# Turning 32x32 blocks on VectorE and the rest by transfers, in place of TensorE transposes, in a FoX and RWKV-7 hybrid layer

## The chip, the core and the metric

The kernel runs on one core of a Trainium2 chip. The core's engines are named as in the profile: PE (TensorE; PEld is its weight load), DVE (VectorE), ACT (ScalarE), POOL (GpSimd) and SP (SyncE, which here only issues DMA transfers). 16 DMA engines move data between DRAM and the core's SBUF. The metric is the device time of one execution in microseconds (us), as a median of several; lower is better.

## The reference

One layer for 256 tokens of width 4096, in float32. One projection feeds two groups of heads and a gate, and their gated outputs go through a second projection into a LayerNorm residual:

```python
proj = jnp.einsum('bsd,dc->bsc', x, w_in)            # 4096 -> 16,592 columns
# 16 FoX heads of 128: causal softmax attention with a forget gate
logits = jnp.einsum('bhqd,bhkd->bhqk', qb, kf) + cb[..., :, None] - c[..., None, :]
out = jnp.einsum('bhqk,bhkd->bhqd', softmax(where(causal, logits, -inf)), vf)
# 32 RWKV-7 heads of 64: r, k, v are shifted by a token (a lerp with the token before), then per frame
sa = jnp.einsum('bhvk,bhk->bhv', state, a_t)
state = state * w_t[:, :, None, :] + sa[..., None] * b_t[:, :, None, :] + v_t[..., None] * k_t[:, :, None, :]
y_t = jnp.einsum('bhvk,bhk->bhv', state, r_t)
# GroupNorm of y per head, plus the bonus sum(r*k*r_k) * v
h = jnp.concatenate([fox_out, rwkv_out], -1) * silu(z)
x = layernorm(ALPHA * x + h @ w_out)
```

## The kernel before

**The projections.** The tokens are the matmul's stationary operand, in two halves of 128 (x, split into a high and a low part in fp32r), and the weights stream through. A weight tile w_q is 128x1024 float32, 512 KB: two steps of the contraction for 512 columns. SP fetches it (`fetch`, L215; 4 buffers), ACT rounds it to its high part (L138; 4 buffers), DVE subtracts to get the low part (L139; 3 buffers), and PE runs 12 matmuls on it (L144 to L146: high times high, low of x times high, high of x times low). Sixteen such tiles make a block of 512 columns for all 256 tokens, accumulated in two PSUM banks `acc`. The 16 groups of heads are taken as 8 pairs n, each with four blocks b: block 0 holds r and k of both groups of the pair, block 1 v of RWKV and v of FoX, blocks 2 and 3 q, k and the two gates of the even and of the odd group. The output projection (L784 to L786) is built alike from 128 tiles `wo`.

**The side work.** Everything else is written as generators that are resumed in slots: `slot()` is called every six matmuls, twice in a weight tile, and lets each of them go on to its next `yield`. `wait(n)` lets n slots pass, so the table `W` fixes how far apart in PE's stream the steps of a chain stand. The framework then orders each engine's instructions by when its own cost model has them ready, with program order as priority; `keep_in_program_order` pins one. Each engine and SP's DMA queue works its list strictly in order, so an instruction that waits holds those behind it.

**Where tiles are turned.** A block comes out of PE with tokens on the partitions; the recurrence and attention want channels there. `unload` (L721) turns the copy `bk` by TensorE transposes against the identity into PSUM tiles `tr` (L735), four per group, and ACT and DVE read those: `shifted` (L270) makes r, k and v with the token shift, L746 and L749 take q and k of a FoX head, `silu2` (L347) the gates. v is made a second time with tokens on the partitions (`vs`, L829 to L831 and L493 to L495) by a copy through DRAM one row apart and three POOL operations.

**The recurrence** (`rwkv`, L476) of a pair: Gram products `gp` (L488); their masked parts go through DRAM (nd, L509, eight transfers, and Nb, L510, two of 512 KB) into the layout of a triangular solve on DVE of 31 rows, each one product and one reduction (L536, L539); BK, the update's factors, is turned by eight transposes `tp` (L525) and copied by ACT (L526); the inverse goes back through DRAM (td, T; L545, L547), and a chunked sweep of PE steps follows. `bon`, the bonus, is multiplied by v (L517) ahead of the solve.

**Attention** (`fox`, L663): scores (L672, L673), softmax on DVE and ACT in `lg` (L678 to L682), three transposes `fpt` of the probabilities (L686), a copy to `pT` (L688), the product with v (L692).

Of the kernel before, what the change touches and what calls it, by code (L numbers as in the profile page):

```python
# [22 lines left out]
C = 64  # L23
NCH = S // C
# [15 lines left out]
BACK = 10  # L40
ROWS = 1
LAG = 2
BLOCKS = [[(0, 0), (1, 0), (0, 1), (1, 1)], [(2, 0), (2, 1)], [(3, 0), (4, 0), (5, 0), (6, 0)], [(3, 1), (4, 1), (5, 1), (6, 1)]]
W = {"fo": 3, "vs": 2, "np": 6, "gp": 5, "tp": 4, "d1": 8, "d2": 12, "xp": 3, "fs": 4, "fp": 5}
NB = D // OB

# [2 lines left out]
B = 32  # L49
# [33 lines left out]
def layer(ctx: ExitStack, tc: tile.TileContext, xt, xtok, w_lora, w_main, muv, w_o, up, par, mulora, fbias, lng, lnb, cst, out):  # L83
    nc = tc.nc
# [8 lines left out]
    def pst(name):  # L93
        return ps.tile([P, 512], F32, tag="ps", name=name)
# [37 lines left out]
    def column(name, i):  # L132
        return prm[:, PAR.index(name), i : i + 1]
# [124 lines left out]
    def t256(tag, name, bufs=1):  # L258
        return rp.tile([P, S], F32, tag=tag, name=name, bufs=bufs)
# [7 lines left out]

    vv = {}

    def shifted(p, n, i):  # L270
        name = f"s{n}_{i}"
        if n == 2:
            if i % 2 == 0:
                vv[i // 2] = rp.tile([P, 2, S], F32, tag="s2", name=name)
            r = vv[i // 2][:, i % 2, :]
        else:
            r = t256(f"s{n}", name, 2)
        lerp(p, prm[:, 7 + n, i : i + 1], omm[:, n, i : i + 1], r)
        return r

# [66 lines left out]
    def silu2(z, key):  # L347
        th = t256("zt", key + "t")
        nc.scalar.activation(th, z, AF.Tanh, scale=0.5)
        sz = t256("sz" + key[0], key + "s", 2 if key[0] == "r" else 1)  # L350
        nc.vector.scalar_tensor_tensor(sz, th, 1.0, z, ALU.add, ALU.mult)
        szs[key] = sz

    def gate(y, key, k):
        far = k < FAR
# [17 lines left out]
    def flat(t):  # L373
        return t.rearrange("p a b -> p (a b)")
# [3 lines left out]
    bks = {}  # L378
    muvs = {}
    turned = set()  # L380
    pairs = {}
    done = set()
    prepared = set()
# [91 lines left out]

    def rwkv(n):  # L476
        i0 = 2 * n
        while i0 + 1 not in prepared or n not in vv:
            yield
        q = pairs[n]  # L480
        lc, BK, lt, bon = q["lc"], q["BK"], q["lt"], q["bon"]
# [7 lines left out]
        v = vv[n]  # L489
# [27 lines left out]
        nc.vector.tensor_tensor(flat(bon), flat(bon), flat(v), ALU.mult)  # L517
        for u in range(2):
            nc.scalar.activation(bon[:, u], bon[:, u], AF.Identity, bias=column("gn_bias", i0 + u))
        yield from wait(W["tp"])  # L520
        BKt = rp.tile([P, 2, NCH, P], F32, tag="shl", name=f"BKt{n}")
        for u in range(2):
            tp = pst(f"tp{n}_{u}")
            for c in range(NCH):
                nc.tensor.transpose(tp[:, c * P : (c + 1) * P], BK[:, u, c, :], ident)  # L525
# [8 lines left out]
        for t, s in enumerate(range(B - 2, -1, -1)):  # L534
            w = B - 1 - s
            first = nc.vector.tensor_tensor(prod[:, :, :, s + 1 :], nb[:, :, s : s + 1, s + 1 :].to_broadcast([P, 2, NJ, w]), xc[:, :, :, s + 1 :], ALU.mult)  # L536
            if not t:
                tc.keep_in_program_order(first)
            nc.vector.tensor_reduce(xc[:, :, :, s : s + 1], prod[:, :, :, s:], AX.X, ALU.add)  # L539
            if t % ROWS == ROWS - 1:  # L540
                yield
        td = dram.tile([2, 4, NCH, B, B], F32, tag="td", name=f"td{n}", bufs=2)
# [120 lines left out]
    def fox(i, q, k, vt):  # L663
# [13 lines left out]
        for m, blk in enumerate((slice(0, 1), slice(1, 3))):  # L677
            nc.vector.scalar_tensor_tensor(lg[:, blk, :], spv[:, blk, :], ct[:, m * NF + i : m * NF + i + 1], nb[:, blk, :], ALU.add, ALU.add)  # L678
            nc.vector.tensor_reduce(st[:, m : m + 1], lg[:, blk, :], AX.XY, ALU.max, negate=True)
            nc.scalar.activation(lg[:, blk, :], lg[:, blk, :], AF.Exp, bias=st[:, m : m + 1], accum_out=st[:, 2 + m : 3 + m])  # L680
            nc.vector.reciprocal(st[:, 4 + m : 5 + m], st[:, 2 + m : 3 + m])
            nc.vector.tensor_scalar(lg[:, blk, :], lg[:, blk, :], st[:, 4 + m : 5 + m], None, ALU.mult)  # L682
        yield from wait(W["fp"])
        pt = pst(f"fpt{i}")
        for m in range(3):
            nc.tensor.transpose(pt[:, m * P : (m + 1) * P], lg[:, m, :], ident)  # L686
        pT = rp.tile([P, 3 * P], F32, tag="nb", name=f"pT{i}")
        nc.scalar.copy(pT, pt[:, : 3 * P])  # L688
        yield from wait(W["fo"])
        op = pst(f"fop{i}")  # L690
        f = slice(i % 2 * P, i % 2 * P + P)
# [22 lines left out]

    zero = rp.tile([1, 2 * P], F32, tag="prod", name="zero")
    nc.gpsimd.memset(zero, 0.0)
    vds = [dram.tile([S + 1, 2 * P], F32, name=f"vd{j}") for j in range(2)]
    for vd in vds:
        nc.sync.dma_start(out=vd[0:1], in_=zero)

    def unload(n, b, bk, vt):  # L721
        yield from wait(LAG)
        if b == 0:
            while n and 2 * n - 1 not in prepared:
                yield
        elif b == 2:
            while n and n - 1 not in done:
                yield
        fq = fk = None
        cols = BLOCKS[b]  # L730
        for h in range(len(cols) // 2):
            tr = pst(f"tr{n}_{b}_{h}")
            for t in range(2):
                for m in range(2):
                    nc.tensor.transpose(tr[:, t * S + m * P : t * S + (m + 1) * P], bk[:, m, (2 * h + t) * P : (2 * h + t + 1) * P], ident)  # L735
            for t in range(2):
                p = tr[:, t * S : (t + 1) * S]
                j, u = cols[2 * h + t]
                i = 2 * n + u
                if j < 3:  # L740
                    rk[i, j] = shifted(p, j, i)
                elif j == 3:
                    while i and i - 1 not in foxed:
                        yield
                    fq = t256("fq", f"fq{i}")
                    nc.scalar.mul(fq, p, FOX_SCALE)  # L746
                elif j == 4:
                    fk = t256("fk", f"fk{i}")
                    nc.scalar.copy(fk, p)  # L749
                    side(fox(i, fq, fk, vt))  # L750
                else:
                    silu2(p, f"fr"[j - 5] + str(i))
            yield
        unloading.clear()

    def get_h(k):
        assert k in kept_h
# [54 lines left out]
    for n in range(G // 2):  # L812
        for b in range(4):
# [12 lines left out]
            if b == 1:  # L826
# [10 lines left out]
            unloading.append(n)  # L837
            side(unload(n, b, bk, vt))

    closed.append(1)  # L840
    oacc = {}
# [174 lines left out]
```

## Time and profile before

| | |
|---|---|
| median of 3 runs | 1968.98 us (1968.77 to 1969.45) |
| the profiled execution's own time | 1967.9 us |
| its span, first to last instruction | 1966.1 us |
| mean granted TensorE clock | 0.999 |
| PE busy | 1955.8 us, 99% |
| DVE busy | 1351.5 us, 69% |
| ACT busy | 999.5 us, 51% |
| POOL busy | 81.0 us, 4% |
| DMA: bytes, packets | 392.86 MB, 146,383 |

How to read the rows that follow. A row of groups has line, engine, operation, output<-inputs and shapes, count, then busy time and mean ns of one, then idle time before it with what ended it. A row of a tile's view has count, then shortest, median and longest ns. A row of waits has who waited for whom, us in total, times, the longest. A time line has start and duration in us, and in brackets the idle time before it. A row of stretches has each engine's busy time and count, the granted clock, the mean busy share of the 16 DMA engines, and GB/s. The ends of matmuls are modelled; starts are recorded.

### The profile page before, as it was taken

What the parts mean: (1) busy time and instruction counts of PE and PEld (TensorE: products, weight loads), DVE (VectorE), ACT (ScalarE), POOL (GpSimd) and SP (SyncE); (2) the same over time, 40 slices, a digit from 0 to 9 for tenths busy, and PEclk for the clock granted to TensorE, in tenths of its full rate; (3) what the DMA queues carried; (4) which work ended last, traced back from release to release, by engine and by line L of the source; (5) the groups of instructions that cost most, each with busy time, mean ns of one, the idle gap of its engine ahead of it and who ended that gap; (6) DMA issues with size and microseconds to landing.
All of it is one profiled execution on the core that took longest, in us unless ns stands there. A gap on an engine that the chain in (4) does not pass through costs nothing.

```text
span 1966.1 us, 28320 instructions
## 1 busy us (share of the span) xinstructions
PE 1955.8 (99%) x10377; PEld 1608.1 (82%) x10377; DVE 1351.5 (69%) x2168; ACT 999.5 (51%) x1509; POOL 81.0 (4%) x111
## 2 busy tenths in 40 slices
PE   9999999999999999999999999999999999999998
PEld 8888788878887888788878887888788878888886
DVE  6688576857685768576857685778576856755555
ACT  6544564456445644564456445644564454444332
POOL 0110001000100010001000100010001000000000
PEclk9999999999999999999999999999999999999999
DMA  9566567656665666566656665676566787866664
GB/s 337 153 204 192 174 192 201 198 172 192 194 198 178 192 201 201 168 191 196 200 176 193 198 195 177 192 209 187 174 190 198 242 281 240 250 200 200 193 199 165
DMA packets 146383, 392.86 MB, mean 200 GB/s; under 512 B 32642, under 2 KB 48020, under 8 KB 146244
## 3 DMA queue, kind: packets, MB, share of 16 engines
q1 hardware_dynamic: 145812, 390.63, 65.4%
q8 instruction: 81, 1.33, 0.3%
q14 instruction: 58, 0.48, 0.1%
q10 hardware_dynamic: 432, 0.43, 0.1%
HBM read 374.98 MB, written 16.01 MB: 199 GB/s over the span
## 4 chain that ended last, share of the span: by engine, by line
PE 98%; DVE 1%; ACT 0%; issue 0%; ACTq 0%; DVEq 0%
PE acc L144 24%; PE acc L146 24%; PE acc L145 24%; PE oacc L784 6%; PE oacc L786 6%; PE oacc L785 6%; PE tr L735 1%; PE yp L634 1%; PE gp L488 1%; PE up L609 1%; PE rh L582 1%; PE sp L618 0%; PE accl L146 0%; PE accl L144 0%; PE accl L145 0%; PE tp L525 0%
## 5 line engine op out<-in xcount | busy, mean ns | idle before, releaser
L539 DVE TENSOR_REDUCE xc<-prod 128x8 f32<-128x16 f32 (+30 forms) x248 | 73.1, 295 | 6.0
L536 DVE TENSOR_TENSOR prod<-Nb,xc 128x8 f32<-128x8 f32 (+30 forms) x248 | 72.3, 292 | 7.1
L139 DVE TENSOR_TENSOR w_11l<-w,w_11h 128x1024 fp32r<-128x1024 f32 x31 | 37.9, 1223 | 39.0 <-ACT w_11h L138 20.4
L139 DVE TENSOR_TENSOR w_6l<-w,w_6h 128x1024 fp32r<-128x1024 f32 x31 | 38.0, 1226 | 37.0 <-ACT w_6h L138 17.5
L139 DVE TENSOR_TENSOR w_1l<-w,w_1h 128x1024 fp32r<-128x1024 f32 x31 | 37.9, 1223 | 35.9 <-PE acc L146 35.7
L139 DVE TENSOR_TENSOR w_0l<-w,w_0h 128x1024 fp32r<-128x1024 f32 x31 | 37.9, 1223 | 33.8 <-PE acc L146 22.3
L138 ACT CAST w_1h<-w 128x1024 fp32r<-128x1024 f32 x31 | 32.7, 1055 | 55.4 <-PE acc L145 37.6
L139 DVE TENSOR_TENSOR w_3l<-w,w_3h 128x1024 fp32r<-128x1024 f32 x31 | 37.8, 1221 | 31.8 <-PE acc L146 31.8
L138 ACT CAST w_2h<-w 128x1024 fp32r<-128x1024 f32 x31 | 32.7, 1056 | 48.8 <-PE acc L145 42.1
L138 ACT CAST w_11h<-w 128x1024 fp32r<-128x1024 f32 x31 | 32.5, 1050 | 46.5 <-DMA w<-in_w_main_dram 29.2
L138 ACT CAST w_0h<-w 128x1024 fp32r<-128x1024 f32 x31 | 32.7, 1055 | 43.5 <-PE acc L145 34.9
L139 DVE TENSOR_TENSOR w_2l<-w,w_2h 128x1024 fp32r<-128x1024 f32 x31 | 37.9, 1222 | 22.6 <-PE acc L146 22.4
L144 PE MATMUL acc<-w_4h,x 128*128 128x512 f32 x124 | 53.0, 427 | 0.0
L139 DVE TENSOR_TENSOR w_15l<-w,w_15h 128x1024 fp32r<-128x1024 f32 x31 | 37.9, 1221 | 21.6 <-PE acc L146 20.2
L139 DVE TENSOR_TENSOR w_9l<-w,w_9h 128x1024 fp32r<-128x1024 f32 x31 | 38.0, 1226 | 21.1 <-ACT pT L688 15.3
L138 ACT CAST w_13h<-w 128x1024 fp32r<-128x1024 f32 x31 | 32.7, 1054 | 37.5 <-DMA w<-in_w_main_dram 21.6
L139 DVE TENSOR_TENSOR w_14l<-w,w_14h 128x1024 fp32r<-128x1024 f32 x31 | 38.0, 1225 | 19.7 <-PE acc L146 9.0
L138 ACT CAST w_4h<-w 128x1024 fp32r<-128x1024 f32 x31 | 32.7, 1055 | 36.7 <-PE acc L145 36.7
L144 PE MATMUL acc<-w_1h,x 128*128 128x512 f32 x124 | 51.2, 413 | 0.0
L144 PE MATMUL acc<-w_6h,x 128*128 128x512 f32 x124 | 51.2, 413 | 0.0
L144 PE MATMUL acc<-w_2h,x 128*128 128x512 f32 x124 | 51.1, 412 | 0.0
L139 DVE TENSOR_TENSOR w_5l<-w,w_5h 128x1024 fp32r<-128x1024 f32 x31 | 43.5, 1403 | 10.9 <-PE acc L146 10.9
(836 smaller groups left out, 6592.9 us busy)
## 6 DMA issues: line engine op xcount, KB each, us to landing
w<-in_w_main_dram SPq DMA_DIRECT2D x496, 512.0 KB, 3.7
wo<-in_w_o_dram SPq DMA_DIRECT2D x128, 512.0 KB, 3.6
Nb<-nd SPq DMA_DIRECT2D x16, 512.0 KB, 5.8
wr<-in_w_main_dram SPq DMA_DIRECT2D x15, 512.0 KB, 6.4
hd<-hl SPq DMA_DIRECT2D x29, 256.0 KB, 4.4
h<-hd SPq DMA_DIRECT2D x29, 256.0 KB, 6.5
res<-in_xtok_dram SPq DMA_DIRECT2D x16, 256.0 KB, 4.7
xr<-in_xt_dram SPq DMA_DIRECT2D x15, 256.0 KB, 6.4
```

What stands on the lines that cost most here:

```text
L138: nc.scalar.copy(hi[:, :n], src[:, :n])
L139: nc.vector.tensor_tensor(lo[:, :n], src[:, :n], hi[:, :n].bitcast(F32), ALU.subtract)
L144: nc.tensor.matmul(acc[:, :n], xs[k][:, 0, tt], hi[:, o : o + n], start=(k == 0), stop=False)
L145: nc.tensor.matmul(acc[:, :n], xs[k][:, 1, tt], hi[:, o : o + n], start=False, stop=False)
L146: nc.tensor.matmul(acc[:, :n], xs[k][:, 0, tt], lo[:, o : o + n], start=False, stop=(k == KT - 1))
L488: nc.tensor.matmul(gp[u][j][:, c * P : (c + 1) * P], BK[h, u, c, :], lt[j][h, u, c, :], start=True, stop=True)
L536: first = nc.vector.tensor_tensor(prod[:, :, :, s + 1 :], nb[:, :, s : s + 1, s + 1 :].to_broadcast([P, 2, NJ, w]), xc[:, :, :, s + 1 :], ...
L539: nc.vector.tensor_reduce(xc[:, :, :, s : s + 1], prod[:, :, :, s:], AX.X, ALU.add)
L582: nc.tensor.matmul(rh[HALF[j], u * C : (u + 1) * C], lt[j][:, u, c, 0:C], SV[j][:, u, c, :], start=True, stop=True)
L784: nc.tensor.matmul(acc, ht[k][:, 0, tt], hi, start=(k == 0), stop=False)
L785: nc.tensor.matmul(acc, ht[k][:, 1, tt], hi, start=False, stop=False)
L786: nc.tensor.matmul(acc, ht[k][:, 0, tt], lo, start=False, stop=(k == KT - 1))
```

## The change

A 128-wide transpose is taken apart: DVE turns each 32x32 block within its own 32 partitions, and a transfer through DRAM moves the blocks to their places. The new helper `turn` writes a DVE-turned tile to DRAM with four transfers, one for each group of 32 partitions, in runs of 32 floats; reading the DRAM tile with partition = (block, row) gives the turned tile, in rows of 1 KB and more.

```diff
+    def turn(src, name):
+        _, m, cols = src.shape
+        d = dram.tile([cols // B, B, m, 4, B], F32, tag=f"dt{m}_{cols}", name=name, bufs=2)
+        s = src.rearrange("p m (q t) -> p m q t", t=B)
+        for a in range(4):
+            nc.sync.dma_start(out=d[:, :, :, a, :].rearrange("q i m t -> i m q t"), in_=s[B * a : B * (a + 1)])
+        return d
...
+    def turned_back(d):
+        return d.rearrange("(u b) i m a t -> u (b i) (m a t)", b=4).rearrange("u p s -> p u s")
```

**Projected blocks** 0, 2 and 3 go this way, except blocks 2 and 3 of the last pair, which keep the PE transposes. Block 3 starts 13 slots later (`BEHIND`). After the read-back, three slots (`LAND`) pass before r and k are shifted, two before attention starts; each group's r and k are read back together.

```diff
+        last = n == G // 2 - 1 and b > 1
+        if b == 3 and not last:
+            yield from wait(BEHIND)
+        if not last:
+            for m in range(2):
+                nc.vector.transpose(bk[:, m, :], bk[:, m, :])
+            yield
+            d = turn(bk, f"bt{n}_{b}")
+            unloading.clear()
+            yield
+        if b == 0:
+            for u in range(2):
                 i = 2 * n + u
+                while n and n - 1 not in bonned:
+                    yield
+                raw = rp.tile([P, 2, S], F32, tag="s2", name=f"raw{i}")
+                nc.sync.dma_start(out=raw, in_=turned_back(d[8 * u : 8 * u + 8]))
+                yield from wait(LAND)
+                for j in range(2):
+                    rk[i, j] = shifted(raw[:, j, :], j, i)
+            return
...
+            for j, t in enumerate((fq, fk, zf, zr)):
+                nc.sync.dma_start(out=t, in_=d[4 * j : 4 * j + 4].rearrange("b i m a t -> (b i) (m a t)"))
+                if j % 2:
+                    yield
+            yield from wait(LAND - 1)
+        nc.scalar.mul(fq, fq, FOX_SCALE)
+        side(fox(i, fq, fk, vt))
+        yield
+        silu2(zf, f"f{i}")
+        silu2(zr, f"r{i}")
```

**v** is no longer shifted a second time: block 1 has no `unload` any more, and the token-major `vs` is turned during the solve (rows 6, 8 and 10: `V_AT`), with UV as scratch. The bonus product and its two ACT operations move from ahead of the solve to its row 14.

```diff
+            if t == V_AT:
+                vst = UV[0].rearrange("p u c v -> p (u c v)").rearrange("p (m q) -> p m q", m=2)
+                for a in range(2):
+                    tc.keep_in_program_order(nc.vector.transpose(vst[:, a, :], vs_[n][:, a, :]))
+            if t == V_AT + 2:
+                vdr = turn(vst, f"vt{n}")
+            if t == V_AT + 4:
+                vv[n] = rp.tile([P, 2, S], F32, tag="s2", name=f"vv{n}")
+                nc.sync.dma_start(out=vv[n], in_=turned_back(vdr))
```

**BK** is turned in place and through DRAM, two slots from the transposes to the writes and two to the read; the number of slots to the solve stays as it was.

```diff
+        for u in range(2):
+            tc.keep_in_program_order(nc.vector.transpose(flat(BK[:, u]), flat(BK[:, u])))
+        yield from wait(2)
+        bd = turn(BK.rearrange("p u c t -> p (u c) t"), f"BKt{n}")
+        yield from wait(2)
         BKt = rp.tile([P, 2, NCH, P], F32, tag="shl", name=f"BKt{n}")
-        for u in range(2):
-            tp = pst(f"tp{n}_{u}")
-            for c in range(NCH):
-                nc.tensor.transpose(tp[:, c * P : (c + 1) * P], BK[:, u, c, :], ident)
-            nc.scalar.copy(flat(BKt[:, u]), tp)
-        yield from wait(W["d1"])
+        nc.sync.dma_start(out=BKt.rearrange("p u c t -> p (u c t)"), in_=bd.rearrange("q i g a t -> (q i) (g a t)"))
+        yield from wait(W["d1"] - 4)
```

**Attention's probabilities** of heads 0 to 13 are turned the same way.

```diff
+        if i < G - 2:
+            nc.vector.transpose(flat(lg), flat(lg))
         yield from wait(W["fp"])
+        if i < G - 2:
+            ld = turn(lg, f"fpt{i}")
+            yield from wait(2)
...
+        if i < G - 2:
+            nc.sync.dma_start(out=pT, in_=ld.rearrange("q i m a t -> (q i) (m a t)"))
```

The gates' results now overwrite their inputs (`silu2`), since these lie in SBUF and no longer in PSUM.

More of the change, by code (lines that the diff above doesn't have):

```diff
@@ L268, in layer @@
     vv = {}
-    def shifted(p, n, i):
[L271 to L277, printed above, removed]
+    def turn(src, name):
[5 more added lines that the diff above has]
+        return d
+    def shifted(p, n, i):
+        r = t256(f"s{n}", f"s{n}_{i}", 2)
         lerp(p, prm[:, 7 + n, i : i + 1], omm[:, n, i : i + 1], r)
@@ L380, in layer @@
     turned = set()
+    bonned = set()
     pairs = {}
@@ L477, in rwkv @@
         i0 = 2 * n
-        while i0 + 1 not in prepared or n not in vv:
+        while i0 + 1 not in prepared or n not in vs_:
             yield
@@ L728, in unload @@
                 yield
[L729 to L738, printed above, removed]
-                i = 2 * n + u
[L740 to L752, printed above, removed]
-            yield
@@ new lines, in unload @@
+        i = 2 * n + b - 2
+        while i and i - 1 not in foxed:
+            yield
+        fq, fk = t256("fq", f"fq{i}"), t256("fk", f"fk{i}")
+        zf, zr = t256("szf", f"zf{i}"), t256("szr", f"zr{i}", 2)
+        if last:
+            for h, pair in enumerate(((fq, fk), (zf, zr))):
+                tr = pst(f"tr{h}")
+                for t in range(2):
+                    for m in range(2):
+                        nc.tensor.transpose(tr[:, t * S + m * P : t * S + (m + 1) * P], bk[:, m, (2 * h + t) * P : (2 * h + t + 1) * P], ident)
+                for t in range(2):
+                    nc.scalar.copy(pair[t], tr[:, t * S : (t + 1) * S])
+                yield
+            unloading.clear()
+        else:
+            for j, t in enumerate((fq, fk, zf, zr)):
[3 more added lines that the diff above has]
+            yield from wait(LAND - 1)
```

34 lines of the change are left out of this document (19 added, 15 removed).

## The prediction

> **What bounds the kernel now.** I read the page first: busy time, then the chain that ended last; after that PE's own waits.
>
> ```profile
> span 1966.1 us, 28320 instructions
> PE 1955.8 (99%) x10377; PEld 1608.1 (82%) x10377; DVE 1351.5 (69%) x2168; ACT 999.5 (51%) x1509; POOL 81.0 (4%) x111
> PE 98%; DVE 1%; ACT 0%; issue 0%; ACTq 0%; DVEq 0%
> ```
>
> ```profile
> PE zp L921 <- DVE zd L909: 1.4, 1, 1.4
> ...
> PE fpt L686 <- DVE lg L682: 0.3, 1, 0.3
> ```
>
> PE is busy for 99% of the span, 98% of the chain runs over it, and its longest wait, 1.4 us, lies in the tail; the one on something this change touches is 0.3 us. A busy PE could still be one that is slowly fed, so I looked at the pitch of its matmuls around a group of transposes in the time line.
>
> ```profile
> 319.92 0.39 PE L146 MATMUL acc<-w_1l,x 128*128 128x512 f32 x1
> 320.15 0.60 PE L735 MATMUL tr<-cs,bk 128*128 128x128 f32 x4
> 320.51 0.48 PE L144 MATMUL acc<-w_1h,x 128*128 128x512 f32 x1
> 320.82 0.39 PE L145 MATMUL acc<-w_1h,x 128*128 128x512 f32 x1
> 321.05 0.40 PE L146 MATMUL acc<-w_1l,x 128*128 128x512 f32 x1
> ```
>
> Starts lie 0.23 us apart where nothing else stands between them (320.82 to 321.05). Without the four transposes the L144 matmul would start at 320.15 and the L145 one at 320.38; it starts at 320.82. Four transposes cost PE 0.44 us. The chain of waits says the same, and 0.87 us for the eight of BK:
>
> ```profile
> 320.32 0.44 PE tr L735 x4
> ...
> 336.62 0.87 PE tp L525 x8
> ```
>
> So whatever PE no longer does comes off the end, as long as the split weights still reach it in time. That condition is the whole question.
>
> **What is removed.** The counts are those of the tiles' views:
>
> ```profile
> L735 PE MATMUL tr<-cs,bk x224: 270/272/330, 76.9 to 1597.2; 128*128 128x128 f32 x112
> L525 PE MATMUL tp<-cs,BK x64: 270/272/273, 139.8 to 1517.7; 128*128 128x128 f32 x64
> L686 PE MATMUL fpt<-cs,lg x48: 271/273/327, 185.9 to 1616.9; 128*128 128x128 f32 x48
> ```
>
> Of the 224 tr transposes 16 stay (blocks 2 and 3 of the last pair): 208 / 4 x 0.44 = 22.9 us. All 64 of BK go: 8 x 0.87 = 7.0 us. Of the 48 for probabilities the last two heads keep 6: 42 x 0.11 = 4.6 us. Together 34.5 us of PE, all on the chain. ACT also loses copies out of PSUM: it is at 51%, so this counts as nothing.
>
> **What DVE gets.** Per pair (two heads of each kind): three projected blocks and BK, each two transposes of 128x512; v, two of 128x256; two heads of probabilities, one of 128x384 each. The one transpose in the trace is narrow; beside it stand other DVE operations.
>
> ```profile
> L566 DVE STREAM_TRANSPOSE X<-T 32x256 f32<-32x256 f32 x32 | 13.9, 435 | 0.6
> L461 DVE TENSOR_TENSOR BK<-k,eI 64x256 f32<-64x256 f32 x32 | 13.3, 416 | 0.2
> L452 DVE TENSOR_TENSOR shl<-sb,shl 128x512 fp32r<-128x512 f32 x16 | 11.0, 689 | 0.2
> L266 DVE SCALAR_TENSOR_TENSOR s<-tr,prm,s 128x255 f32<-128x255 f32 x48 | 22.3, 478 | 14.7 <-ACT s L265 14.4
> ```
>
> At 256 columns a transpose costs what an elementwise operation costs (435 against 416 ns), so at 512 I take 0.69 us; the other end is twice 435, 0.87 us. Per pair: 8 x 0.69 + 2 x 0.44 + 2 x 0.56 = 7.5 us, less the two v shifts that go (2 x 0.48): +6.6 us, or +8 us at the other end. Now the room, by block of 16 weight tiles of one pair:
>
> ```profile
> core 0: us, PE busy (x) PEld busy (x) DVE busy (x) ACT busy (x) POOL busy (x), PEclk, DMA share, GB/s
> 268.30:317.40 49.10, 49.10 (x224) 40.70 (x223) 36.05 (x50) 28.01 (x42) 0.22 (x2) 1.00 0.62 187
> 317.40:366.60 49.20, 49.20 (x246) 40.74 (x245) 36.58 (x70) 21.84 (x28) 6.57 (x4) 1.00 0.72 210
> 366.60:415.80 49.20, 49.20 (x290) 40.44 (x289) 35.49 (x65) 23.59 (x36) 0.59 (x2) 1.00 0.69 201
> 415.80:464.90 49.10, 49.10 (x321) 39.49 (x320) 31.08 (x52) 29.92 (x57) 1.18 (x4) 1.00 0.53 164
> ...
> 348.60:382.30 33.70, 33.70 (x155) 27.95 (x154) 32.05 (x85) 15.92 (x23) 0.00 (x0) 1.00 0.64 187
> ```
>
> A pair takes 196.6 us and would take 192.3 (34.5 / 8 off). DVE then has 139.2 + 6.6 = 146 of 192, 76%. The last row is the triangular solve: DVE at 95%. Into that stretch come the v transposes (0.9), block 2's two (1.4) and the bonus product that was before it (0.7), 3.0 us; out of it goes the softmax of the even head (about 2 us), as attention now starts some seven slots (a slot is half a weight tile, 6 x 0.23 = 1.4 us) later. I cost DVE at nothing: the cover is the 0.23-us pitch of PE with splits running ahead. If the softmax stayed, 35.0 us would have to go into 33.7.
>
> **What the DMA rings and SP's queue get.** A turn writes the 32x32-turned tile to DRAM in runs of 128 bytes, four transfers, and reads it back whole, in one to four transfers. Per pair: 4 x 4096 runs (blocks 0, 2, 3 and BK), 2048 (v), 2 x 1536 (probabilities), 21,504 runs or 2.75 MB, written and read once. The trace has such runs in the writes of nd and the reads of T; these are the queue lines of the page, then of 332.3 to 335.8 us, then of 386.2 to 389.0 us:
>
> ```profile
> q1 hardware_dynamic: 145812, 390.63, 65.4%
> ```
>
> ```profile
> DMA packets 1038, 0.63 MB, mean 179 GB/s; under 512 B 910, under 2 KB 910, under 8 KB 1038
> ...
> q1 hardware_dynamic: 1038, 0.63, 73.6%
> ```
>
> ```profile
> DMA packets 955, 0.51 MB, mean 182 GB/s; under 512 B 855, under 2 KB 855, under 8 KB 954
> ...
> q1 hardware_dynamic: 954, 0.50, 59.8%
> ```
>
> Large packets cost 0.654 x 16 x 1966 / 390.63 MB = 52.7 ps a byte, 0.216 us for 4 KB. First window: 0.736 x 16 x 3.5 = 41.2 us of engine time less 128 x 0.216 leaves 13.6 us for 910 small ones, 15 ns each. Second: 26.8 less 99 x 0.216 leaves 5.4 for 855, 6 ns. The upper bound is all packets of the first window alike: 40 ns. I take 15, the window of writes. A pair then adds 21,504 x 15 / 16 = 20.2 us of each engine for writing and 2.75 MB x 52.7 / 16 = 9.1 us for reading; the share goes from 64% (mean of the four rows) to (125.8 + 29.3) / 192.3 = 81%; at 6 ns 75%, at 40 ns 98%.
>
> The Trainium skill speaks against this ("DMA: Bandwidth & Descriptors", Specifications: below 512 bytes a transfer is off line rate, the engine does read-modify-write). By that rule each run would be moved twice, 30 ns; the 15 ns measured here on such writes would already hold it. What 30 ns would do is rival one.
>
> All transfers share SP's queue with the weight fetches. Does a burst there reach PE? The trace has one, the solve's factors, in the SP, ACT and DVE time lines and the views of w_11l and w_12l:
>
> ```profile
> 331.35 0.33 SPq L215 DMA_DIRECT2D w<-in_w_main_dram  x1
> 331.94 3.78 SPq L509 DMA_DIRECT2D nd<-gb  x8
> 335.88 1.54 SPq L510 DMA_DIRECT2D Nb<-nd  x2
> 337.97 14.07 SPq L215 DMA_DIRECT2D w<-in_w_main_dram  x7
> ```
>
> ```profile
> 345.11 1.05 ACT L138 CAST w_11h<-w 128x1024 fp32r<-128x1024 f32 x1 [5.36 <-DMA w<-in_w_main_dram]
> ```
>
> ```profile
> 346.19 1.23 DVE L139 TENSOR_TENSOR w_11l<-w,w_11h 128x1024 fp32r<-128x1024 f32 x1 [3.25 <-ACT w_11h L138]
> 347.47 1.23 DVE L139 TENSOR_TENSOR w_12l<-w,w_12h 128x1024 fp32r<-128x1024 f32 x1
> ```
>
> ```profile
> L146 PE MATMUL acc<-w_11l,x x4: 389/389/389, 350.1 to 352.1; 128*128 128x512 f32 x4
> ```
>
> ```profile
> L146 PE MATMUL acc<-w_12l,x x4: 389/389/389, 352.8 to 354.8; 128*128 128x512 f32 x4
> ```
>
> For 6.6 us (331.35 to 337.97) no weight is asked for, then 1 MB of Nb is ahead of the next one, 3.5 us of the rings. ACT stands 5.36 us, DVE 3.25, and the split is still done at 347.4, 2.7 us before PE takes it. A block's turn is of that size: issue 4 x 0.42 = 1.7 us (the L509 row with its gaps: 3.78 / 8 = 0.47), a wait for the last write, the read; rings 4096 x 15 / 16 = 3.8 us and 1.7 us. The wait is bounded by a like pair, vd written and vs read back:
>
> ```profile
> SPq L831 <- DMA vd<-bk: 12.1, 8, 2.3
> ```
>
> 1.5 us each. Behind that waiting read stands the next weight fetch, for which ACT, then DVE, then PE wait in turn. Turns away from the solve's burst I cost at nothing: covered as w_11 is. The one of BK comes right behind it: its transposes take the place of the tp matmuls (336.62), its writes follow two slots later, about 339.3, so one or two fetches go first and the next two come behind 3.8 + 1.7 = 5.5 us of rings. Those splits would be some 4 us ahead, as w_12l is (done at 348.7, taken at 352.8); at worst 5.5 - 4 = 1.5 us of PE per pair. (Had it caught w_11 itself, 5.5 - 2.7 = 2.8.) I take 0.4 us per pair, 3 us in all, since part of the 5.5 us runs while PE's other tiles are used.
>
> **The sum.** The profiled execution took 1967.9 us. 1967.9 - 34.5 + 3 = 1936.4. It lies 1.1 us under the median of the runs, 1968.98, so the forecast is 1937 us.
>
> **Rivals.** One, slower: the small runs are dearer than the two windows say, and BK's turn holds up the weights each pair. Its place is the weights behind BK's writes; its price per pair is run price x 4096 / 16 + 1.7 - 4.0. The gain is gone at 34.5 / 8 = 4.3 us per pair, that is from 26 ns a run. At 40 ns: 7.9 x 8 = 63 us, 1997 us. For it: 40 ns is not excluded, and longer trains than nd's 128 runs a transfer are not in the trace. Against it: both windows give half or less. By the skill's rule above, 30 ns: 5.4 x 8 = 43 us, 1978 us.
>
> Two, late weights in part: the worst cases at 15 ns, 1.5 to 2.8 us per pair, 12 to 22 us returned: 1946 to 1957 us. For it: the turn really is queued behind the burst. Against: the order of SP's queue is planned, and fetches may go first.
>
> Three, DVE in the solve: 35.0 us into 33.7, 1.3 x 8 = 10 us: 1945 us. For it, 95% busy; against it, later softmax and splits ahead by 3 to 4 us.
>
> Four, no change: the splits, not PE, set the pace once PE has less to do, and PE's gaps grow by what it saves: 1968 us. Against it: DMA 64%, DVE 71% and ACT 53% in the four rows, and no wait of PE there.
>
> **Chances.** Forecast with its neighbourhood (1934 to 1943) 0.60; two 0.13; three 0.08; four 0.06; one 0.13. A measurement of this kernel tells about 0.2%, 4 us, from no change. Faster: 0.60 + 0.13 + 0.08 = 0.81; same 0.06; slower 0.13. The range holds the first three: 1932 (34.5 us, nothing returned, and 2 us for PE's gaps around the groups) to 1960 us.
>
> **What would show it.** Right: PE's matmuls at 0.23 us with no tr or tp between them, PE's waits still short and in the tail, PE at 99% of a span of about 1935, DMA near 75 to 81%, 128x512 transposes at about 0.7 us. Wrong: PE waiting for splits (rows at L139 or L138 among its waits) around 340 to 360 us of a pair and behind each block's end (rival one or two; the queue share of a window of turn writes tells the price of a run), or DVE at 100% in the solve with w splits directly ahead of PE (three), or a pitch above 0.23 us (four).

## The result and the profile after

The changed kernel takes 2053.3 us (median of four runs, 2051.4 to 2054.4) against 1968.9 us for the kernel before on the same chip: 1.0429 times as long, interval 1.0416 to 1.0441. The forecast was 1937 us. The page of the changed kernel, the lines that answer to those shown of before:

```profile
span 2049.6 us, 28216 instructions
...
PE 1963.8 (96%) x10063; PEld 1592.2 (78%) x10063; DVE 1396.4 (68%) x2242; ACT 969.9 (47%) x1455; POOL 84.6 (4%) x111
...
DMA packets 328241, 434.03 MB, mean 212 GB/s; under 512 B 198370, under 2 KB 228852, under 8 KB 328100
...
q1 hardware_dynamic: 327668, 431.81, 69.9%
...
PE 79%; DVE 11%; DMA 5%; issue 2%; ACT 2%; SPq 1%; ACTq 0%; DVEq 0%
```

The transposes are gone (314 fewer PE instructions) and PE is still busy 8 us longer, in a span 83.5 us longer; a fifth of the chain no longer runs over PE (DVE 11%, DMA 5%). PE's waits (line waited for, us in total, times, longest) name the engines:

```profile
PE acc L148 <- DVE w_11l L141: 33.3, 8, 4.8
PE acc L146 <- ACT w_5h L140: 14.7, 6, 2.8
PE acc L146 <- ACT w_4h L140: 11.1, 1, 11.1
PE acc L146 <- ACT w_12h L140: 4.1, 6, 0.8
```

All are splits of weights, where before PE waited for none of them over 0.2 us. I also took the distance between the starts of each two neighbouring weight matmuls, less the usual 227 ns: 16 distances of over 1 us make 65 us, and what lies between 60 ns and 1 us grew by 43 us, from 21 to 65; the distances that held the transposes gave back 29 us (tr 19, tp 6, fpt 4). 65 + 43 - 29 = 79 of the 83.5 us.

The single wait of 11.1 us, at w_4h, lies in the first pair: ACT stands 7.8 us before a copy of SV to UV (L575), whose input DVE makes behind the solve's last row, and the cast stands behind that copy. Most of the other long waits stand at two places of each pair's 206 us. The first is w_11 of block 2. SP's, ACT's, DVE's and PE's time lines there (start, length):

```profile
352.41 0.54 SPq L513 DMA_DIRECT2D Nb<-nd  x1
353.13 6.27 SPq L277 DMA_DIRECT2D BKt<-BK  x4
359.44 1.50 SPq L217 DMA_DIRECT2D w<-in_w_main_dram  x2
```

```profile
364.29 1.05 ACT L140 CAST w_11h<-w 128x1024 fp32r<-128x1024 f32 x1 [5.54 <-DMA w<-in_w_main_dram]
```

```profile
359.80 1.23 DVE L141 TENSOR_TENSOR w_10l<-w,w_10h 128x1024 fp32r<-128x1024 f32 x1 [1.50 <-PE acc L148]
360.94 0.17 DVE L537 TENSOR_TENSOR prod<-Nb,xc 128x8 f32<-128x8 f32 x1
...
372.31 1.22 DVE L141 TENSOR_TENSOR w_11l<-w,w_11h 128x1024 fp32r<-128x1024 f32 x1
```

```profile
373.58 1.22 PE L148 MATMUL acc<-w_11l,x 128*128 128x512 f32 x2 [4.81 <-DVE w_11l L141]
```

The fetch of w_11 stands behind BK's four writes, but its data are cast by 365.3 us. DVE takes the split 7 us later, because in its list w_11l comes behind 20 of the solve's 31 rows and the two v transposes. In the kernel before it came ahead of the first row. In the program's own order it follows the first row. That the planner (the framework's ordering of each list by its own cost model) put it behind row 20 because it reckoned with a late fetch, behind BK's writes, is my reading. It fits that the split stands ahead of the first row (e3) or behind five at most (e2, e7, e8) once BK's writes are off the fetches' queue or gone; in e5, with BK's writes on that queue, it stands ahead of the first row all the same.

The second place is block 1 (w_5, w_6). SP's time line:

```profile
282.51 2.18 SPq L217 DMA_DIRECT2D w<-in_w_main_dram  x2
284.80 2.82 SPq L277 DMA_DIRECT2D fpt<-lg  x4
287.72 0.57 SPq L277 DMA_DIRECT2D bt<-bk  x1
290.07 0.33 SPq L706 DMA_DIRECT2D pT<-fpt  x1
290.46 2.10 SPq L277 DMA_DIRECT2D bt<-bk  x3
297.88 0.33 SPq L366 DMA_DIRECT2D hd<-hl  x1
298.26 0.43 SPq L217 DMA_DIRECT2D w<-in_w_main_dram  x1
```

No weight is asked for from 284.7 to 298.3 us: eight writes and a read, and then 5 us in which SP stands before hd<-hl, the write of attention's gated output, which now comes after the turned probabilities' way through DRAM.

Last, PE's clock. The next two windows of the changed kernel lie behind a wait of 2.23 us (at 303.9) and one of 4.97 us (at 373.6); the column ahead of the last two is the granted clock:

```profile
304.80:306.80 2.00, 1.96 (x5) 1.39 (x5) 2.00 (x6) 1.83 (x3) 0.00 (x0) 0.50 0.84 342
374.00:377.00 3.00, 3.00 (x8) 2.32 (x8) 2.86 (x7) 0.00 (x0) 0.00 (x0) 0.50 0.66 186
```

At 0.50 there are 8 matmuls in 3 us, where 13 go at 227 ns. Behind the 16 long waits this made 0.7 to 2.2 us each, by an estimate from the starts some 25 of the 43 us of short excess.

### The profile page after: what moved, and what is told of

Its sections match the earlier page's. It is cut to its first block, busy times and chain, and to the rows that moved or that the text cites. A ratio compares the mean times of both kernels' runs of the same rounds, so it can differ in the third digit from the quotient of the medians.

```text
span 2049.6 us, 28216 instructions
## 1 busy us (share of the span) xinstructions
PE 1963.8 (96%) x10063; PEld 1592.2 (78%) x10063; DVE 1396.4 (68%) x2242; ACT 969.9 (47%) x1455; POOL 84.6 (4%) x111
## 2 busy tenths in 40 slices
DMA packets 328241, 434.03 MB, mean 212 GB/s; under 512 B 198370, under 2 KB 228852, under 8 KB 328100
## 3 DMA queue, kind: packets, MB, share of 16 engines
q1 hardware_dynamic: 327668, 431.81, 69.9%
## 4 chain that ended last, share of the span: by engine, by line
PE 79%; DVE 11%; DMA 5%; issue 2%; ACT 2%; SPq 1%; ACTq 0%; DVEq 0%
PE acc L146 19%; PE acc L148 18%; PE acc L147 18%; PE oacc L831 6%; PE oacc L833 6%; PE oacc L832 6%; DMA w<-in_w_main_dram 4%; DVE xc L540 3%; DVE prod L537 3%; SPq L277 1%; PE yp L649 1%; PE gp L492 1%; PE up L624 1%; PE rh L597 1%; DVE w_11l L141 1%
## 5 line engine op out<-in xcount | busy, mean ns | idle before, releaser
L148 PE MATMUL acc<-w_11l,x 128*128 128x512 f32 x124 | 54.1, 449 | 33.3 <-DVE w_11l L141 33.3
L146 PE MATMUL acc<-w_5h,x 128*128 128x512 f32 x124 | 54.0, 436 | 14.7 <-ACT w_5h L140 14.7
L141 DVE TENSOR_TENSOR w_4l<-w,w_4h 128x1024 fp32r<-128x1024 f32 x31 | 38.0, 1225 | 38.7 <-PE acc L148 32.6
L141 DVE TENSOR_TENSOR w_12l<-w,w_12h 128x1024 fp32r<-128x1024 f32 x31 | 37.9, 1222 | 37.3 <-ACT w_12h L140 35.6
L146 PE MATMUL acc<-w_4h,x 128*128 128x512 f32 x124 | 51.1, 412 | 11.1 <-ACT w_4h L140 11.1
L141 DVE TENSOR_TENSOR w_8l<-w,w_8h 128x1024 fp32r<-128x1024 f32 x31 | 37.9, 1223 | 33.1 <-PE acc L148 18.5
L140 ACT CAST w_15h<-w 128x1024 fp32r<-128x1024 f32 x31 | 32.6, 1052 | 57.6 <-PE acc L147 20.6
L148 PE MATMUL acc<-w_5l,x 128*128 128x512 f32 x124 | 52.7, 425 | 2.4 <-DVE w_5l L141 2.4
L146 PE MATMUL acc<-w_12h,x 128*128 128x512 f32 x124 | 50.8, 410 | 4.2 <-ACT w_12h L140 4.1
L146 PE MATMUL acc<-w_11h,x 128*128 128x512 f32 x124 | 51.7, 417 | 1.6 <-ACT w_11h L140 1.6
L140 ACT CAST w_8h<-w 128x1024 fp32r<-128x1024 f32 x31 | 32.6, 1051 | 43.0 <-PE acc L147 32.4
L684 POOL TENSOR_SCALAR_AFFINE_SELECT nb<-nb 128x128 f32<-128x128 f32 x32 | 22.9, 716 | 701.0 <-DMA nb<-ncd 420.0
```

The source lines that it names most:

```text
L140: nc.scalar.copy(hi[:, :n], src[:, :n])
L141: nc.vector.tensor_tensor(lo[:, :n], src[:, :n], hi[:, :n].bitcast(F32), ALU.subtract)
L146: nc.tensor.matmul(acc[:, :n], xs[k][:, 0, tt], hi[:, o : o + n], start=(k == 0), stop=False)
L148: nc.tensor.matmul(acc[:, :n], xs[k][:, 0, tt], lo[:, o : o + n], start=False, stop=(k == KT - 1))
L684: nc.gpsimd.affine_select(out=nb[:, m, :], in_=nb[:, m, :], compare_op=ALU.is_ge, fill=NEG, base=0, pattern=[[-1, P]], channel_multiplier=1)
```

## The experiments

Two theories. "Order of the lists": each engine and queue works through a fixed list; splits and fetches were put behind work that itself waits. "Queues full of runs" (rival one, in a milder form): the 128-byte runs hold up the weights wherever they stand. All ratios are against the kernel before on the same chip.

**e1: pin the solve's rows.**

```diff
-            if not t:
-                tc.keep_in_program_order(first)
+            tc.keep_in_program_order(first)
```

> Every row of the solve is pinned behind what is traced before it on VectorE, so that the split w_11l stands behind 1 row of the solve and not behind 20; transfers, their number and their order on SyncE's queue are left as they are. Theory 'order of the lists': TensorE's wait for w_11l (33.3 us in 8 waits, 5.0 us a pair) falls under 8 us in all, the 3.4 us of clock 0.5 behind each goes with it, and the time falls by 40 to 55 us, to 1998 to 2013 us. Theory 'queues full of 128-byte runs': the weights land late whatever VectorE does; the wait turns from VectorE to ScalarE or the transfer, keeps at least half of its length, and the time stays at 2035 to 2053 us.

2011.4 us, 1.0230 [1.0212, 1.0248]: 42 us less, with the same transfers. DVE's time line, block 2:

```profile
352.44 1.22 DVE L141 TENSOR_TENSOR w_11l<-w,w_11h 128x1024 fp32r<-128x1024 f32 x1 [3.44 <-ACT w_11h L140]
```

The split follows its cast, and the wait there is gone. The waits at w_11l left in this run (8.7 us, a little over the 8 that were expected at most) are those of block 3, behind the solve's end, which came later: its last row starts at 401.4 us, against 385.4 in the changed kernel. New is w_4 (11 us), whose fetch stands behind a block's writes that wait for DVE.

**e2: BK by PE again.** The four lines of BK's turn replaced by the two transposes into PSUM and copies of before.

> The factors BK are turned by TensorE and copied by ScalarE as in the kernel before; all other turns stay with VectorE and transfers. Theory 'order of the lists': w_11l stands behind 5 rows of the solve and not 20, its wait goes, the waits at w_5h and w_6h stay; 7 us of TensorE come back: 2053 - 54 + 7 = 2006 us (2000 to 2015). Theory 'queues full of runs': 8192 of some 41,000 short runs a pair go, the rest stays, so about a fifth of the 84 us goes: 2036 us (2030 to 2045).

2003.9 us, 1.0184 [1.0169, 1.0200]. w_11l stands behind five rows, its wait is gone; w_5 keeps its own (17.5 us in 7). This is what the first theory expected, not the second. (The expectation took 41,000 for the short runs of a pair, which is all packets; of the 21,504 runs that the turns write, BK's are 4096, again about a fifth.)

**e3: the turns' writes from ACT's queue.**

```diff
-            nc.sync.dma_start(out=d[:, :, :, a, :]...
+            nc.scalar.dma_start(out=d[:, :, :, a, :]...
```

> The four writes of each turn are issued from ScalarE's queue instead of SyncE's; the same bytes in the same 128-byte runs on the same engines. Theory 'order of the lists': fetches of weights no longer stand behind the writes, w_11l stands behind 1 row of the solve, its wait goes and most of those at w_5h and w_6h: 1975 to 2005 us. Theory 'queues full of runs': the fetches start earlier but land as late; 2040 to 2055 us. A third way: ScalarE loses 0.6 us for each of 176 writes, is late with casts, and the time is 2060 us or more with TensorE waiting for w_...h.

2040.7 us, 1.0366 [1.0346, 1.0387]. The time lies in the range of the second theory (2040 to 2055), but the place is that of the third way, at less than its 2060 us: ACT's casts now stand behind the issues of the writes. ACT's waits:

```profile
ACT w_9h L140 <- DMA BKt<-BK: 58.2, 6, 12.3
ACT w_4h L140 <- DMA bt<-bk: 57.3, 11, 6.7
```

The run moves the wait to another list, and does not decide between the theories.

**e4: hd's write from GpSimd's queue.**

```diff
-            nc.sync.dma_start(out=hd[k], in_=flat(hl).bitcast(F32))
+            nc.gpsimd.dma_start(out=hd[k], in_=flat(hl).bitcast(F32))
```

> Only the write of hl to hd (it waits 5.3 us at the median on SyncE for VectorE, 60.5 us in all) is issued from GpSimd's queue; the solve's order on VectorE is left, w_11l behind 20 rows. Theory 'order of the lists': the 14 us without a fetch of weights in block 1 end, the waits of 2.2 to 2.9 us at w_5h and w_6h in six pairs go with their time at clock 0.5, and the waits at w_11l stay: 2053 - 6 x (2.5 + 1.7) = 2028 us (2020 to 2038). Theory 'queues full of runs': those waits are the turns' own and stay: 2048 to 2055 us.

2025.7 us, 1.0291 [1.0276, 1.0307]. The rows w_5h and w_6h are gone from PE's waits, and w_11l is the longest:

```profile
PE acc L148 <- DVE w_11l L141: 41.2, 14, 6.0
```

One kind of small transfer that waits, ahead of the fetches, cost 28 us.

**e5: the kernel before with BK's turn alone.**

> The kernel before with BK's turn alone (two transposes on VectorE, four writes, one read); blocks, recurrent values and probabilities stay with TensorE. w_11l stands ahead of the solve's first row, as before. Theory 'order of the lists': the short runs by themselves do no harm; TensorE loses 64 transposes (6.3 us), no wait over 1 us for a split comes: 1962 us (1957 to 1968). Theory 'queues full of runs': BK's writes, four to seven us for 4096 runs, hold up the weights in each pair, TensorE waits 2 us or more in each: 1980 to 2010 us.

1972.2 us, 1.0022 [1.0013, 1.0032]: between the theories, nearer the first. No split is behind the solve, yet the 6.3 us do not arrive. SP's and ACT's time lines:

```profile
340.48 1.51 SPq L518 DMA_DIRECT2D Nb<-nd  x2
342.51 0.36 SPq L215 DMA_DIRECT2D w<-in_w_main_dram  x1
344.92 4.06 SPq L275 DMA_DIRECT2D BKt<-BK  x4
349.02 1.49 SPq L215 DMA_DIRECT2D w<-in_w_main_dram  x2
```

```profile
354.90 1.05 ACT L138 CAST w_12h<-w 128x1024 fp32r<-128x1024 f32 x1 [5.16 <-DMA w<-in_w_main_dram]
```

Here the data are late: w_12's fetch is issued behind 1 MB of Nb and 4096 runs and lands some 5 us later; PE waits 0.7 to 1.6 us for w_12 in about every second pair.

**e6: e2 and e4 together.**

> BK by TensorE (as in e2) and hd's write on GpSimd's queue (as in e4) together; blocks, recurrent values and probabilities stay turned by VectorE and transfers. Theory 'order of the lists': both places of the loss are gone, what e2 (2004) still waits at w_5h and w_6h (22 us, and 8 x 1.7 us at clock 0.5) goes: 1968 us (1960 to 1980). Theory 'queues full of runs': four fifths of the runs are left, and so is most of what e2 still lost: 1990 to 2004 us.

1974.5 us, 1.0032 [1.0022, 1.0042]: 79 of the 84 us are gone with four fifths of the runs in place. Left are, above all, 7.5 us at w_12h behind the probabilities' writes and 4.7 us once at w_6h.

**e7: weights from GpSimd's queue, all turns on SP.**

> The fetches of weights are issued from GpSimd's queue, everything else stays on SyncE's, with all turns as in the changed kernel; w_11l stands behind 5 rows of the solve. Theory 'order of the lists': no fetch stands behind a write that waits; the waits at w_11l, w_5h, w_6h and w_12h go, and what is left is what the transposes gave: 1940 to 1965 us. Theory 'queues full of runs': fetches start in time and land late, with TensorE waiting for casts that wait for transfers: 2000 us or more. A third way: GpSimd's own list waits (masks, the factors' scaling) and the fetches behind it do: 2000 us or more, with the issue late and not the landing.

2037.1 us, 1.0350 [1.0320, 1.0380]. PE's waits:

```profile
PE fop L715 <- DMA pT<-fpt: 31.1, 11, 7.1
PE acc L146 <- ACT bk L869: 12.3, 8, 4.4
```

This is none of the three expectations: the short runs are all there (328,242 packets), and no wait for a weight is among PE's long ones. PE waits for turned data instead. That its small matmuls stand where the planner expects pT and its like to have come is my reading; that short runs make these data late is not excluded by this run.

**e8: the turns' and hd's writes from GpSimd's queue.**

> The turns' writes and hd's write are issued from GpSimd's queue, fetches of weights and reads stay on SyncE's; w_11l stands behind 5 rows of the solve. Theory 'order of the lists': 1940 to 1975 us, with SyncE never more than 4 us between two fetches in block 1. Theory 'queues full of runs': 2010 us or more, as the runs are the same. A third way: GpSimd takes several us to issue 1024 runs, the turned blocks land late, and TensorE waits for pT or the recurrence ends later: 2000 us or more with short waits for weights.

2012.8 us, 1.0217 [1.0200, 1.0234]. This is the third way, with PE waiting for turned data:

```profile
PE fop L715 <- DMA pT<-fpt: 31.5, 14, 4.1
```

The time lies in the second theory's range too (2010 or more), but with these writes on GpSimd's queue the kernel moved the same bytes in 170,867 packets, not 328,241, so this run tells nothing about short runs.

**e9: only blocks and v turned** (e6 with the probabilities by PE as well).

> Only projected blocks and recurrent values are turned by VectorE and transfers; BK and the probabilities are turned by TensorE, and hd's write is on GpSimd's queue. In e6 the fetch of w_12 stood on SyncE behind the probabilities' writes, which waited for VectorE's lg (397.5, fetches at 400.5 us): those writes are gone. Theory 'order of the lists': the waits at w_12h and for pT go (7.5 + 2.8 us, and 6 x 1.7 us at clock 0.5), 4 us of transposes come back: 1974.5 - 20 + 4 = 1958 us (1950 to 1965), faster than both kernels. A rival, 'each turn's own latency': the blocks' turns alone still cost what they free: 1966 to 1975 us.

1970.9 us, 1.0015 [1.0006, 1.0023]: less gain than the first theory expected, and in the rival's range (1966 to 1975). The waits at w_12h went, but another took their place, on DVE in block 1, behind the second group's decay and key work, which waits for the turned block:

```profile
PE acc L148 <- DVE w_12l L141: 10.6, 7, 1.5
```

**e10: the kernel before with hd's write on GpSimd's queue.**

> The kernel before with only hd's write on GpSimd's queue: what that edit is worth without any turn. Theory 'order of the lists': in before no fetch of weights is late behind it, TensorE waits for no split, so 1968.5 us (1965 to 1971). If the write costs there too, it is part of what e4, e6 and e9 gained: 1955 to 1963 us.

1968.2 us, 1.0000 [0.9991, 1.0009]. The edit itself is worth nothing; the gain in e4 is the changed kernel's own loss.

**e11: e4 with the rows pinned and the probabilities by PE**; blocks, v and BK turned.

> Blocks, recurrent values and BK turned by VectorE and transfers, the probabilities by TensorE, hd's write on GpSimd's queue, and every row of the solve pinned, so that w_11l stands behind 1 row. Theory 'order of the lists': the three places found so far (w_11l behind 20 rows, hd ahead of fetches, the probabilities' writes ahead of w_12) are all out of the way; what is left is e1's wait at w_4h behind the next block's writes (11 us, and 6 x 1.7 us at clock 0.5) and 1.6 us a pair at w_11l: 2011 - 8 x 4.3 - 8 = 1969 us (1960 to 1980).

1986.6 us, 1.0093 [1.0080, 1.0107]. This is 17 us over what was expected. w_4h, 11.8 us as in e1, was in the expectation; new is the w_12l of e9 (11.2 us in 8 waits), which I had not known of, and the rest I have not placed. Still, six sevenths of the short runs are in place here, and the time is 67 us under the changed kernel's.

**e12: e9 with the key work later**, and the first pair's copies of SV behind w_6h.

```diff
+        if u:
+            yield from wait(4)
         k = rt(f"k{i}")
-        nc.vector.tensor_tensor(k, kr, am, ALU.mult)
+        first = nc.vector.tensor_tensor(k, kr, am, ALU.mult)
+        if u:
+            tc.keep_in_program_order(first)
```

> e9 with two changes of order and none of work: the decay and key work of each second group of a pair (k and what follows) is traced four slots later and pinned behind the split w_12l, and in the first pair alone ScalarE's copies of SV to UV are traced two slots later and pinned behind the cast w_6h. In e9 w_12l stands behind 6.9 us of that work on VectorE though its cast ended at 305.6 us, and TensorE waits 1.68 us for it in seven pairs; w_6h stands behind the copies and costs 5.3 us once. Theory 'order of the lists': these eight waits and the half clock behind each (1.7 us) go: 1970.9 - 7 x 3.4 - 7 = 1940 us (1937 to 1952), faster than both kernels. A rival, 'the turns cost what they free whatever the order': the wait moves to w_13l or to the solve, 1962 us or more.

1965.0 us, 0.9985 [0.9976, 0.9994]. The seven waits went; the expected 1940 us did not come, and the time is the rival's (1962 or more). The waits of e9, 1.68 us each by the starts, were not followed by a slow clock (1.00 in the window behind one):

```profile
512.40:515.40 3.00, 3.00 (x14) 2.38 (x14) 3.00 (x5) 0.37 (x1) 0.00 (x0) 1.00 0.64 182
```

so seven waits were worth 7 x 1.68 = 12 us, not 24; and, as the rival had it, a wait moved to the solve: in the first pair w_5l came to stand behind the last row, one wait of 9.2 us.

**e13: e5 with BK's writes after row 6 and its read after row 10**, rows pinned.

> e5 (the kernel before with BK's turn alone, 1972) with BK's writes issued after row 6 of the solve and its read after row 10, instead of directly behind the copies Nb (1 MB); VectorE's transposes of BK stay where they were, and the solve's rows are pinned so that no split of weights falls behind them. In e5 TensorE waits 0.7 to 1.6 us for w_12 in every second pair, whose fetch lands 5 us after its issue behind Nb and 4096 short runs. Theory 'burst': it is the place, two bursts one behind the other; moved, 6.3 us of transposes are won: 1962 us (1958 to 1966). Theory 'runs cost wherever they stand': 1969 to 1975 us.

1967.5 us, 0.9996 [0.9987, 1.0004]: 4.7 us better than e5, no wait for a split over 0.6 us, and the same as before. The place of the burst, together with the pins, was about half of the 10 us by which e5 missed 1962. The time lies between the two theories' ranges. Why only about 1 us of 6.3 is won I can't say: the starts show PE 4 us longer in distances that hold side matmuls, 2 of them at tr, and 1 us in other short distances, with no releaser.

**e14: e12 without the change to the copies, the first pair's rows pinned.**

```diff
-            if not t:
+            if not t or not n:
                 tc.keep_in_program_order(first)
```

> e12 without the change to the copies of SV, but with the solve's rows of the first pair pinned, so that w_5 of its block 3 stands behind 14 rows and not 31; later pairs as e12. In e12 one wait of 9.3 us at w_5l (191.6 us) is left. Theory 'order of the lists': it goes with its half clock: 1965 - 9.3 - 2.5 = 1953 us (1950 to 1958). Rival: the wait moves to w_6h or to the writes of the block's turn behind the rows, as in e9 (5.3 us) or e1 (2.1 us): 1958 to 1963 us.

1953.1 us, 0.9923 [0.9910, 0.9935], as expected. The page, and the longest of PE's waits, which lies in the tail:

```profile
span 1950.9 us, 28331 instructions
...
PE 1939.3 (99%) x10169; PEld 1586.8 (81%) x10169; DVE 1362.6 (70%) x2212; ACT 982.5 (50%) x1485; POOL 92.8 (5%) x140
```

```profile
PE zp L964 <- DVE zd L952: 1.4, 1, 1.4
```

This version beats both kernels: blocks and v turned by VectorE and transfers, BK and the probabilities by PE, hd's write on GpSimd's queue, two pins. It keeps two thirds of the short runs (142,338 packets under 512 bytes, against 198,370 in the changed kernel and 32,642 in the kernel before), and PE waits for no split of weights over 0.4 us: with the lists in this order, that many runs hold up no weight.

**e15: all rows pinned, the turns' writes held behind earlier fetches.**

> e14 with the rows of every pair pinned, and the turns' writes held behind the fetches traced before them (block 2's five slots after its transposes, where e1 had SyncE waiting for VectorE and TensorE 2.1 us a pair at w_4h). Work as in e14. Theory 'order of the lists': every fetch and split stands ahead of what can wait, so no wait over 0.7 us: 1950 us (1946 to 1956). Rival: held writes make the turned blocks late, TensorE waits at fsp or np: 1960 us or more.

1961.2 us, 0.9965 [0.9952, 0.9977]. The expectation is missed by 11 us; the time is the rival's, the place is not: w_11l of block 3 falls behind the end of the pinned solve, 1.4 us in six pairs. More pins are not better.

**e16: e15 with BK turned, late.**

> e15 with BK turned by VectorE and transfers too, its writes after row 6 of the solve and its read after row 10; only the probabilities are left to TensorE. Theories 'order of the lists' and 'burst' together: 6 us less than e15: 1944 us (1940 to 1950). Theory 'runs cost wherever they stand': what BK frees is lost again, e15's time or up to 6 us over it.

1978.8 us, 1.0051 [1.0038, 1.0065], 17 us over e15, where neither theory had it. The time line of SP speaks for the order again:

```profile
343.70 5.52 SPq L277 DMA_DIRECT2D BKt<-BK  x3
349.33 0.65 SPq L217 DMA_DIRECT2D w<-in_w_main_dram  x1
355.11 2.59 SPq L277 DMA_DIRECT2D vt<-UV  x4
357.80 0.56 SPq L217 DMA_DIRECT2D w<-in_w_main_dram  x1
```

SP stands from 350.0 to 355.1 us before v's writes, which wait for DVE's transposes among the rows, and the fetch of w_15 behind them makes PE wait (w_15h 5.9 us in 6 waits). No run takes this apart. No kernel with BK turned got under the kernel before by more than 0.04%, so whether BK's turn can pay in some order is open, as is the whole change's best: no run has all four turns and no late split.

## Why the prediction was wrong, step by step

- "So whatever PE no longer does comes off the end, as long as the split weights still reach it in time." Right, and the condition failed. e14 shows the first half: of the 208 tr transposes, worth 22.9 us in my sum, 15 us came off. The price of a group was right: where four transposes stand alone between weight matmuls, the starts give 0.36 us to the distance that holds them and 0.09 to the one behind it. What the sum left out is what came back: about 4 us as longer distances at gp, np and lp, and another 4 that I have not placed.
- "I cost DVE at nothing: the cover is the 0.23-us pitch of PE with splits running ahead." This step failed most: the overlap was taken for granted. DVE's load was right (1396 us against 1351.5 + 8 x 6.6 = 1404, transposes of 128x512 at 0.66 to 0.71 us); I asked how much DVE does in the solve, not what stands in line there. w_11l was done 2.7 us ahead because it stood before the solve's first row; behind 20 rows it has no cover, and PE waits for it, up to 4.8 us in a pair. e1 pins the rows, with the same work and the same transfers, and is 42 us faster.
- "The order of SP's queue is planned, and fetches may go first." I used the planner as a reason for safety. It placed fetches behind BK's writes and behind hd's write, where these runs show them waiting. e4 puts 28 us on hd alone.
- "Turns away from the solve's burst I cost at nothing: covered as w_11 is." Wrong: 13.6 us pass without a fetch in block 1, against the 6.6 us that the cover had stood. The wait was not for the ring but for a write behind attention's new latency. I counted the turn's transfers, and not the transfers already on the queue that the turn makes late.
- "I take 0.4 us per pair" for BK's turn, at worst 2.8. Placed rightly, sized low even by itself: e5 loses about 10 us against the 1962 expected, 1.3 us a pair. The 0.42 us per issue was 0.58 to 0.71 by the medians of the four kinds of turn, and some issues stood for microseconds (SP's issues, least, median and longest in ns):

```profile
L277 SPq DMA_DIRECT2D bt<-bk x88: 569/576/2197, 79.3 to 1525.5; - x88
L277 SPq DMA_DIRECT2D BKt<-BK x32: 589/668/5617, 145.5 to 1597.5; - x32
```

- "I take 15" ns a run. Right for BK's burst; transfers of the changed kernel from 356.5 to 361.5 us:

```profile
DMA packets 4226, 0.77 MB, mean 153 GB/s; under 512 B 4167, under 2 KB 4167, under 8 KB 4226
...
q1 hardware_dynamic: 4226, 0.77, 96.4%
```

  (0.964 x 16 x 5 - 59 x 0.216) / 4167 = 15 ns. So rival one falls by its own threshold of 26 ns. The Trainium skill's rule on transfers under 512 bytes ("DMA: Bandwidth & Descriptors", Specifications) points to the right sign: 128 bytes at 52.7 ps would be 7 ns; the 30 ns estimated from it are not seen here. Over the whole kernel the share rose to 69.9% and not 81%: 147 us more of each engine where 234 had been worked out, which leaves some 8 ns a run, an estimate with the reads at 52.7 ps a byte.
- Three (DVE in the solve, 1945 us) had the place and the engine, but as a load of 1.3 us a pair; as an order it cost 5. Two had the late data, which e5 shows, at a smaller size. None of the rivals had the order of an engine's list as its mechanism, and the dearest, 1997 us, stayed 56 us short. The view that I named for one and two, PE waiting for splits around 340 to 360 us, is where it came out.
- The price of a wait was taken as its length. In the changed kernel the long waits added the slow clock: some 25 us in all, by the estimate above.

## What to carry to other kernels

When transfers or instructions are added to an in-order list, ask of each that may wait what stands behind it, and where a planner will put the critical work among the new; load and bandwidth with room to spare say nothing of this. Look up the critical item's place in the list (here: behind 0, 1, 5 or 20 rows) before adding up times, and give a transfer that waits for a late producer a queue that carries nothing urgent. A freed engine gains only what its feeders' order lets it take: here 15 of the 34.5 us worked out, with the blocks and v turned and the other two left to PE.

## What was not expected of the hardware

- PE's clock went to 0.50 behind each of the changed kernel's 16 long waits, the shortest of 2.23 us, in an otherwise dense stream. The length alone does not decide it: in e1 six waits of 2.3 to 2.8 us were not followed by a slow clock, and in e5 one of 1.57 us, with a second of 0.7 us close behind it, was. The Trainium skill ("TensorE: Matmul & The Clock Gate", Why this matters for your kernels) advises no gaps of over about 3 us; here 2.23 us was enough. In the traces' clock records the stretches at 0.50 ahead of the tail last 3.4 us or a multiple of it, so where a wait falls may count; no run tests this. The window behind a wait of 2.83 us in e1 (at 1297.3), at 1.00, and the one of e5 at 0.50:

```profile
1298.00:1303.00 5.00, 4.47 (x21) 3.70 (x21) 4.96 (x11) 3.93 (x7) 0.11 (x1) 1.00 0.81 288
158.10:161.50 3.40, 3.40 (x8) 2.73 (x9) 3.06 (x12) 0.97 (x2) 0.00 (x0) 0.50 1.04 417
```

- An issue on SP can take far longer than its median: one of BK's writes took 5.6 us, where the median is 0.67 us. With the writes moved away from the 1 MB of Nb (e13) the longest took 2.7 us. That transfers in flight hold an issue is my reading.
- With the turns' and hd's writes issued from GpSimd's queue, the same bytes moved in about half as many packets (170,867 for the kernel, against 328,241).
